# Moving two matmul operands by an odd number of 16-byte lines against the weight buffers

## The chip, the core and the metric

The kernel runs on one core of a Trainium2 chip. The core has a matrix engine (TensorE, PE in the profile; its weight loads are listed apart as PEld), a vector engine (VectorE, DVE), an activation engine (ScalarE, ACT), and queues that start DMA transfers (the SP queue among them). The on-chip memory, SBUF, has 128 partitions; a tile is given by its first byte in each partition. The metric is the device time of one execution in microseconds; lower is better.

## What is computed

A trunk of two layers on 256 tokens of width 2048: layer 0 mixes tokens by pooling, layer 1 by causal attention over one shared K and V, and both attend to 256 memory tokens. Nearly all the work is in dense projections.

```python
def reference(x, mem, w_in, w_out, w_mem_kv, ln_g, ln_b, pool_w, pool_scale, w_kv_shared):
    h = x
    for i in range(DEPTH):                                   # DEPTH = 2
        if i == N_A_LAYERS:                                  # 1
            k_blocks, v_blocks, k_mean = moba_shared_kv(h, w_kv_shared)
        u = h @ w_in[i]                                      # 2048 x 4096
        branch_in, gate_b, mem_q, gate_m = jnp.split(u, split_at, axis=-1)
        if i < N_A_LAYERS:
            branch = multiscale_pool(branch_in, pool_w[i], pool_scale[i])
        else:
            branch = moba_attention(branch_in, k_blocks, v_blocks, k_mean)
        mem_o = memory_attention(mem_q, mem, w_mem_kv[i])
        mixed = jnp.concatenate([branch * jax.nn.silu(gate_b), mem_o * jax.nn.silu(gate_m)], axis=-1)
        h = layer_norm(DEEPNORM_ALPHA * h + mixed @ w_out[i], ln_g[i], ln_b[i])
    return h
```

## The kernel before

Every fp32 number is split into a high part, rounded to the fp32r format that TensorE takes, and a low part, the remainder; a product is the sum of high times high, high times low and low times high. `split` (lines 70 to 73) makes the two parts: ScalarE writes the high one (line 72) and VectorE subtracts it from the source (line 73).

Weights come as items of 512 KB. SP loads each into one of four `raw` buffers, `split` turns it into one of four `wh` and four `wl` buffers of 128 x 1024, and TensorE consumes these. The order of all items is written out once, and TensorE works through it item by item; loads and splits run a fixed number of items ahead.

A matmul has a stationary operand of 128 x 128, which a weight load brings into the array, and a moving operand of up to 512 columns that streams through it. Each matmul here has a weight load of its own. There are four families that read weight buffers together with one of the activation tiles:

- `proj_t` (line 168): the weights are stationary, the activations `xT` or `memT` move. For each of 16 blocks it issues a matmul of 512 columns with `wh` (high and low activations side by side) and one of 256 columns with `wl`. This is the bulk of the kernel.
- `proj_n` (line 194): the activations are stationary (`zT` for the output projections, `memT` for the memory values, `xT` for the shared values), the weights move, 512 columns at a time, in groups of three.
- `pool_mix` (line 564): the weights are stationary, `zT` moves, 256 columns.
- `last` (line 732), for the last output projection: `zT` is stationary, and weights that were split early into `kept` move.

```python
                        if k < KT - 1:
                            mm(acc[n], h[:, kk, s], mov[:, k], k == 0, False)
                        mm(acc[n][:, :T], l[:, kk, s], mov[:, k, :T], False, False)
...
                        mm(acc[t], xh, h[:, kk], first, False)
                        mm(acc[t], xh, l[:, kk], False, False)
                        mm(acc[t], xl, h[:, kk], False, last)
```

(The first three lines are those of `proj_t`, the others those of `proj_n`; `h` and `l` are views of `wh` and `wl`.)

`xm` (line 56) is one region that holds `xT` and `memT`, and later, when these are no longer needed, `kept` and the high and low weights of the shared values (which lie in the place of `memT`). So in the trace `xm` stands for `xT`, `memT` and `kept` alike. All slices that the matmuls take begin at a multiple of 512 bytes from the start of their tile, so the distance between two operands, modulo 512 bytes, is that of their tiles. In the program as built, before the change, the first bytes modulo 512 are: `wh`, `wl`, `raw`, `kept`, `zT` and the attention tiles (`kk`, `qq`, `vv`, `ph`, `pl`) 128; `xT` and `memT` 288, because of `SHIFT = 40` (40 floats, 160 bytes). Counted in lines of 16 bytes, `zT` is level with the weights and `xT` and `memT` lie 10 lines behind them.

Of the kernel before, what the change touches and what calls it, by code (L numbers as in the profile page):

```python
# [12 lines left out]
F32R = mybir.dt.float32r  # L13
# [4 lines left out]
P = 128  # L18
T = 256
D = 2048  # L20
KT = D // P
# [11 lines left out]
BLK = 1024  # L33
RAW_BUFS = 4
WARM = 8
SHIFT = 40
W_BUFS = 4
WARM = 8
SHIFT = 40
LD = 4  # L40
LEAD = 3
LD0 = 8
# [4 lines left out]
def trunk(ctx: ExitStack, tc: tile.TileContext, a: dict, out: bass.AP):  # L47
    nc = tc.nc
    ctx.enter_context(tc.manual_schedule())
    sb = ctx.enter_context(tc.tile_pool(name="sb", bufs=1))  # L50
# [1 line left out]

    xm = sb.tile([P, 2 * KT * 2 * T + 128], F32R, name="xm")
    KX = KT * 2 * T
    xT, memT = (xm[:, SHIFT + i * KX:SHIFT + (i + 1) * KX].rearrange("p (k t) -> p k t", k=KT) for i in range(2))
    kept = [xm[:, i * KX:(i + 1) * KX].rearrange("p (k n) -> p k n", k=KT) for i in range(2)]
    zT = sb.tile([P, KT, 2 * T], F32R, name="zT")  # L60
    res = sb.tile([P, 2, D], F32, name="res")
    ident = mask = psc = eps_t = stats = None

# [189 lines left out]
    def heads_tile(name):  # L253
        return sb.tile([P, 4, 2 * T], F32R, name=name)
# [202 lines left out]
    def fresh(key, make):  # L457

        tiles = []

        def g():
            if not tiles:
                tiles.append(make())
                st[key] = tiles[0]
            return tiles[0]
        return g
# [189 lines left out]
    for grp in range(3):  # L656
        k = fresh("k", lambda: heads_tile("kk"))
# [205 lines left out]
```

## Time and profile before

| | us |
|---|---|
| median of 3 runs | 822.37 (822.33 to 822.89) |
| the profiled execution, its own time | 823.66 |
| its span, first to last instruction | 821.9 |
| TensorE busy | 812.0 |
| VectorE busy | 558.5 |
| ScalarE busy | 396.0 |

The span is what the trace shows; the time of the profiled execution has 1.76 us around it. A matmul's record lasts longer than its share of TensorE, since matmuls overlap: what one costs in a stream is the distance from its start to the start of the next.

### The profile page before, as it was taken

To read this page: it belongs to the slowest core of one execution; us is meant where nothing else is said; L and a number is where in the kernel's file an instruction comes from. 1 tells how busy PE (TensorE), PEld (TensorE's weight loads), DVE (VectorE), ACT (ScalarE), POOL (GpSimd) and SP (SyncE) were. 2 spreads that over 40 slices of the span, in tenths; PEclk is the share of its full clock that TensorE was granted. 3 is DMA by queue.
4 is the path that set the end of the run, shared out by engine and by line. 5 is a ranking of instruction groups with operands and counts; after the bars stand their busy time and mean duration, and the time that the engine had idled before them with its cause. 6 is when DMAs were issued, how large, how long until landed. Compare 5 with 4: busy or idle time off the path is not lost.

```text
span 821.9 us, 11533 instructions
## 1 busy us (share of the span) xinstructions
PE 812.0 (99%) x4444; PEld 702.3 (85%) x4444; DVE 558.5 (68%) x794; ACT 396.0 (48%) x578; POOL 0.2 (0%) x4
## 2 busy tenths in 40 slices
PE   9999999999999999999999999999999999999996
PEld 6888898898888888888898888888888888888885
DVE  5686668657957555697667667566765667658746
ACT  6564545545545434445465445454554445545520
POOL 0000000000000000000000000000000000000000
PEclk9999999999999999999999999999999999999998
DMA  8866555557558666676654554656555555637842
GB/s 324 302 232 205 168 165 180 180 163 227 180 176 292 207 201 192 199 237 197 201 157 152 189 170 157 206 158 198 179 166 168 182 188 167 209 127 232 278 130 103
DMA packets 47164, 159.15 MB, mean 194 GB/s; under 512 B 5375, under 2 KB 7167, under 8 KB 46847
## 3 DMA queue, kind: packets, MB, share of 16 engines
q1 hardware_dynamic: 45792, 155.21, 58.0%
q10 hardware_dynamic: 1316, 3.19, 1.0%
q8 instruction: 35, 0.57, 0.3%
q14 instruction: 21, 0.17, 0.1%
HBM read 156.28 MB, written 2.10 MB: 193 GB/s over the span
## 4 chain that ended last, share of the span: by engine, by line
PE 98%; DVE 1%; DMA 0%; ACT 0%; issue 0%; DVEq 0%; SPq 0%
PE acc L68 89%; PE o L68 4%; PE s L68 2%; PE pt L68 2%; PE pt L363 0%; DMA raw<-in_w_mk 0%; PE pt L313 0%; DVE res L806 0%; PE pt L638 0%; PE o L638 0%; DVE res L787 0%; DVE stats L745 0%; DVE res L744 0%; ACT wh L72 0%; DVEq L859 0%
## 5 line engine op out<-in xcount | busy, mean ns | idle before, releaser
L68 PE MATMUL acc<-xm,wh 128*128 128x512 f32 x1344 | 468.7, 395 | 0.5 <-ACT wh L72 0.5
L73 DVE TENSOR_TENSOR wl<-raw,wh 128x1024 fp32r<-128x1024 f32 (+2 forms) x250 | 295.0, 1186 | 150.0 <-ACT wh L72 149.1
L68 PE MATMUL acc<-xm,wl 128*128 128x256 f32 x1344 | 363.3, 280 | 0.0
L72 ACT ACTIVATE wh<-raw 128x1024 fp32r<-128x1024 f32 (+2 forms) x250 | 255.3, 1028 | 187.3 <-PE acc L68 133.3
L68 PEld LDWEIGHTS acc<-xm,wh 128*128 128x128 f32 x1344 | 248.3, 189 | 49.8 <-ACT wh L72 1.5
L68 PEld LDWEIGHTS acc<-xm,wl 128*128 128x128 f32 x1344 | 253.6, 189 | 7.4 <-DVE wl L73 0.4
L68 PE MATMUL acc<-wh,zT 128*128 128x512 f32 x448 | 140.0, 390 | 0.0
L68 PEld LDWEIGHTS acc<-wh,zT 128*128 128x128 f32 x448 | 84.1, 188 | 17.3
L68 PE MATMUL acc<-wl,zT 128*128 128x512 f32 x224 | 87.2, 389 | 0.0
L68 PE MATMUL acc<-xm 128*128 128x512 f32 x288 | 65.8, 389 | 0.0
L68 PEld LDWEIGHTS acc<-xm 128*128 128x128 f32 x288 | 54.1, 188 | 11.2
L73 DVE TENSOR_TENSOR xm<-raw,xm 128x1024 fp32r<-128x1024 f32 (+2 forms) x41 | 47.7, 1171 | 20.6 <-ACT xm L72 20.4
L221 ACT ACTIVATE fold<-acc 128x256 f32<-128x256 f32 x72 | 27.7, 385 | 62.3 <-PE acc L68 61.1
L72 ACT ACTIVATE xm<-raw 128x1024 fp32r<-128x1024 f32 (+2 forms) x41 | 41.3, 1014 | 19.6 <-PE acc L68 9.8
L68 PEld LDWEIGHTS acc<-wl,zT 128*128 128x128 f32 x224 | 42.1, 188 | 8.5
L222 DVE TENSOR_TENSOR fold<-acc,fold 128x256 f32<-128x256 f32 x72 | 29.4, 418 | 5.4 <-ACT fold L221 5.4
L72 ACT ACTIVATE zT<-zf 128x256 fp32r<-128x256 f32 x32 | 12.9, 414 | 39.6 <-DVE zf L283 35.3
L68 PE MATMUL acc<-xm,zT 128*128 128x256 f32 (+1 forms) x144 | 22.6, 318 | 0.0
L68 PEld LDWEIGHTS acc<-xm,zT 128*128 128x128 f32 x144 | 20.7, 190 | 1.9
L68 PE MATMUL acc<-wh,xm 128*128 128x512 f32 x64 | 21.6, 403 | 0.0
L72 ACT ACTIVATE ph<-pt 128x384 fp32r<-128x384 f32 (+1 forms) x20 | 10.7, 535 | 22.2 <-PE pt L363 13.5
L73 DVE TENSOR_TENSOR zT<-zf,zT 128x256 fp32r<-128x256 f32 x32 | 12.8, 422 | 9.7 <-ACT zT L72 9.7
(124 smaller groups left out, 503.6 us busy)
## 6 DMA issues: line engine op xcount, KB each, us to landing
raw<-in_w_in SPq DMA_DIRECT2D x128, 512.0 KB, 3.5
raw<-in_w_out SPq DMA_DIRECT2D x64, 512.0 KB, 4.3
raw<-in_w_sk SPq DMA_DIRECT2D x24, 512.0 KB, 4.5
raw<-in_w_sv SPq DMA_DIRECT2D x24, 512.0 KB, 3.3
raw<-in_w_mv SPq DMA_DIRECT2D x14, 512.0 KB, 5.6
raw<-in_w_mk SPq DMA_DIRECT2D x12, 512.0 KB, 3.3
raw<-in_xT SPq DMA_DIRECT2D x4, 512.0 KB, 4.8
res<-in_x ACTq DMA_DIRECT2D x2, 1024.0 KB, 5.4
```

Source lines behind the costliest of these rows:

```text
L68: nc.tensor.matmul(o, l, r, start=start, stop=stop)
L72: nc.scalar.activation(hi, src, AF.Copy)
L73: nc.vector.tensor_sub(lo, src, f(hi))
L221: nc.scalar.activation(dst, acc[:, T:], AF.Copy)
L222: nc.vector.tensor_add(dst, acc[:, :T], dst)
```

## The change

```diff
-SHIFT = 40
+LINE = 4
+KEPT = 8
+SHIFT = KEPT + 44
@@
     xT, memT = (xm[:, SHIFT + i * KX:SHIFT + (i + 1) * KX].rearrange("p (k t) -> p k t", k=KT) for i in range(2))
-    kept = [xm[:, i * KX:(i + 1) * KX].rearrange("p (k n) -> p k n", k=KT) for i in range(2)]
-    zT = sb.tile([P, KT, 2 * T], F32R, name="zT")
+    kept = [xm[:, KEPT + i * KX:KEPT + (i + 1) * KX].rearrange("p (k n) -> p k n", k=KT) for i in range(2)]
+    zT = sb.tile([P, KX + 2 * LINE], F32R, name="zT")[:, LINE:LINE + KX].rearrange("p (k t) -> p k t", k=KT)
```

`zT` gets a border of 16 bytes on both sides, so it begins at 144 modulo 512, and every tile that is allocated after it (`raw`, `wh`, `wl`, the attention tiles, the constants) lies 32 bytes further on: 160. `kept` moves by 32 bytes along with them, to 160. `xT` and `memT` move by 48 bytes, to 336. The result, in lines of 16 bytes:

| operand | against the weights before | after |
|---|---|---|
| `xT`, `memT` | 10 lines behind | 11 lines behind |
| `zT` | level | 1 line ahead |
| `kept` | level | level |
| attention tiles | level among themselves | level among themselves |
| `xT` against the shared values' weights in `memT`'s place | level | level |

No instruction is added, removed or moved on any engine: the rows of the program, apart from line numbers, are the same, with the same waits.

## Rows read from the trace of the kernel before

**Rows 1.** The page: its head, part 1, part 4 by engine.
```profile
span 821.9 us, 11533 instructions
...
PE 812.0 (99%) x4444; PEld 702.3 (85%) x4444; DVE 558.5 (68%) x794; ACT 396.0 (48%) x578; POOL 0.2 (0%) x4
...
PE 98%; DVE 1%; DMA 0%; ACT 0%; issue 0%; DVEq 0%; SPq 0%
```

**Rows 2.** Groups by form: count, busy us, mean ns, idle before, releaser.
```profile
L68 PE MATMUL acc<-xm,wh 128*128 128x512 f32 x1344 | 468.7, 395 | 0.5 <-ACT wh L72 0.5
L68 PE MATMUL acc<-xm,wl 128*128 128x256 f32 x1344 | 363.3, 280 | 0.0
L73 DVE TENSOR_TENSOR wl<-raw,wh 128x1024 fp32r<-128x1024 f32 x234 | 284.7, 1223 | 145.2 <-ACT wh L72 144.3
...
L68 PE MATMUL acc<-wh,zT 128*128 128x512 f32 x448 | 140.0, 390 | 0.0
L68 PE MATMUL acc<-wl,zT 128*128 128x512 f32 x224 | 87.2, 389 | 0.0
...
L68 PE MATMUL acc<-wh,xm 128*128 128x512 f32 x64 | 21.6, 403 | 0.0
...
L68 PE MATMUL acc<-wl,xm 128*128 128x512 f32 x32 | 12.6, 393 | 0.0
...
L68 PE MATMUL acc<-xm,zT 128*128 128x256 f32 x96 | 11.7, 283 | 0.0
...
L68 PE MATMUL acc<-xm,zT 128*128 128x512 f32 x48 | 11.0, 389 | 0.0
...
L68 PE MATMUL o<-zT,wh 128*128 128x256 f32 x24 | 4.5, 283 | 0.0
```

**Rows 3.** Timeline of PE, 6 to 9 us: start, length, what.
```profile
6.16 0.63 PE L68 MATMUL acc<-xm,wh 128*128 128x512 f32 x1
...
8.72 0.63 PE L68 MATMUL acc<-xm,wh 128*128 128x512 f32 x1
```

**Rows 4.** Timeline of PE in `proj_t`, 641 to 646 us.
```profile
641.13 0.39 PE L68 MATMUL acc<-xm,wh 128*128 128x512 f32 x1
641.36 0.28 PE L68 MATMUL acc<-xm,wl 128*128 128x256 f32 x1
...
645.98 0.39 PE L68 MATMUL acc<-xm,wh 128*128 128x512 f32 x1
```

**Rows 5.** Timeline of the weight loads, same stretch.
```profile
641.13 0.19 PEld L68 LDWEIGHTS acc<-xm,wl 128*128 128x128 f32 x1
641.36 0.19 PEld L68 LDWEIGHTS acc<-xm,wh 128*128 128x128 f32 x1
```

**Rows 6.** Timeline of PE in the output projection of layer 0, `zT` stationary.
```profile
269.78 0.39 PE L68 MATMUL acc<-wh,zT 128*128 128x512 f32 x1
...
274.99 0.39 PE L68 MATMUL acc<-wh,zT 128*128 128x512 f32 x1
```

**Rows 7.** Timeline of PE in `pool_mix` (`zT` moves), 256 to 258 us.
```profile
256.69 0.40 PE L68 MATMUL o<-zT,wh 128*128 128x256 f32 x2
...
257.77 0.40 PE L68 MATMUL acc<-wh,zT 128*128 128x512 f32 x1
```

**Rows 8.** Timeline of PE in the shared values, `xT` stationary, 508 to 530 us.
```profile
508.03 21.95 PE L68 MATMUL acc<-xm 128*128 128x512 f32 x96
529.81 0.39 PE L68 MATMUL acc<-xm,wh 128*128 128x512 f32 x1
```

**Rows 9.** Timeline of PE in the memory values, `memT` stationary, 14 to 19 us.
```profile
14.53 0.40 PE L68 MATMUL o<-wh,xm 128*128 128x512 f32 x1
...
18.73 0.39 PE L68 MATMUL acc<-xm,wh 128*128 128x512 f32 x1
```

**Rows 10.** Windows: busy us and counts of PE, PEld, DVE, ACT, POOL; clock, DMA share, GB/s.
```profile
5.00:10.00 5.00, 4.68 (x15) 3.93 (x15) 4.11 (x10) 4.06 (x9) 0.00 (x0) 1.00 0.96 327
10.00:13.00 3.00, 3.00 (x18) 2.65 (x18) 1.24 (x2) 1.69 (x2) 0.00 (x0) 1.00 1.00 406
20.00:52.00 32.00, 32.00 (x162) 26.93 (x161) 23.39 (x29) 17.61 (x21) 0.00 (x0) 1.00 0.77 259
122.00:172.00 50.00, 50.00 (x290) 43.94 (x289) 35.72 (x44) 25.78 (x38) 0.00 (x0) 1.00 0.54 169
262.00:336.00 74.00, 74.00 (x328) 61.23 (x328) 42.90 (x44) 30.09 (x31) 0.00 (x0) 1.00 0.65 203
```

More of the change, by code (lines that the diff above doesn't have):

```diff
@@ L35 @@
 WARM = 8
-SHIFT = 40
+LINE = 4
+KEPT = 8
+SHIFT = KEPT + 44
 W_BUFS = 4
 WARM = 8
-SHIFT = 40
+LINE = 4
+KEPT = 8
+SHIFT = KEPT + 44
 LD = 4
```

## The prediction

> **What bounds the kernel now.** I read the page first: TensorE is busy 812.0 of 821.9 us and 98% of the chain that ended last is TensorE [rows 1]. VectorE and ScalarE wait for it more than it waits for them. So the time is the sum of the distances from one matmul's start to the next, and the only question is what a matmul costs in the stream. The groups by form give the counts, but their mean durations (395 ns for 512 columns) overlap and can't be added [rows 2]; the timeline gives the distances, and I took them over long stretches, because its starts are rounded to 10 ns.
>
> Four families have operands that the change moves against each other, and there each distance is longer than the columns alone explain:
>
> - `proj_t`, 10 lines apart: 14 pairs of 512 + 256 columns from 641.13 to 645.98, 346.4 ns a pair [rows 4].
> - `zT` stationary, level: 23 matmuls of 512 columns from 269.78 to 274.99, 226.5 ns each [rows 6].
> - `pool_mix`, level: nine matmuls of 256 columns from 256.69 to 257.77, 120.0 ns each [rows 7].
> - the memory values, 10 lines apart the other way round: 18 matmuls from 14.53 to 18.73, 233.3 ns each [rows 9].
>
> [...]
>
> The load starts when the matmul before its own starts: 641.13 and 641.36 in both timelines [rows 4, 5]. So one matmul's moving operand and the next one's stationary operand are read at the same time, and all the distances that I have are even numbers of lines (0, 10). [...]
>
> **The change part by part.** Nothing is added, removed or reordered, so the only cost or gain is in these distances, and in what the new addresses do to other engines.
>
> Loads that the change touches: `proj_t` 2 x 1344 = 2688; `zT` stationary 448 + 224, and in `last` 96 + 48, together 816; `pool_mix` 3 groups of 24 + 12 = 108; the memory values 96 under the name `acc` and the same again under `pt` and `o` together, 192 [rows 2]. The shared values stay level and keep their 226.9 ns (96 matmuls from 508.03 to 529.81, three times) [rows 8]; attention stays level too. These are the control.
>
> The trace of before shows no odd distance, so the price there is bounded from both sides. Least: no collision at all, the columns alone. That gives 1344 x 26.4 = 35.5 us, 816 x 13.2 = 10.8 us, 108 x 13.3 = 1.4 us, 192 x 20.0 = 3.8 us, together 51.5 us. Most, on the other side: every load pays what the memory values pay, 20.0 ns, 6.7 ns more than now on 2688 + 816 + 108 = 3612 loads: 24.2 us lost. In the middle lies nothing at all.
>
> I take half of the full gain, 25.8 us. The nearest rows are the even ones, and none of them says which way an odd one goes; but if a collision is two reads in the same set of lines, odd against even is the distance at which the two stay apart when both advance a line in the same time. Against all of it going: the price differs between level and 10 lines the one way but not the other, so the two reads don't keep step exactly, and part of the loads will slide back into step.
>
> [...]
>
> Other engines: the source and target of a split move together by 32 bytes, so VectorE and ScalarE see the same relations as before, except for what is written to `zT`, `xT` and `memT`. I cost that at nothing. An item takes TensorE 8 x 346.4 ns = 2.77 us, and VectorE's share of it is 1.223 us [rows 2]; in the `proj_t` stretch VectorE is busy 35.72 of 50 us and the DMA share is 0.54 [rows 10]. With 8% less time per item these become 77% and 0.58: cover is left. If VectorE were 10% slower on the new addresses, it would still be at 85%. Only the start has no cover: from 5 to 13 us the DMA share is 0.96 to 1.00 [rows 10], so a faster TensorE may wait for data there, and the 8 us give back at most 8% of themselves, 0.6 us. From 20 to 52 us it is 0.77, with room.
>
> The sum stands against the profiled execution's own time: 823.66 - 25.8 = 797.9 us. That execution was 1.29 us above the median of the runs shown, so for the median I say 796.5.
>
> **The rivals.** *All of it goes.* [...] Time 822.4 - 51.5 = 770.9 us.
>
> *Only a little goes* (2 to 13 us): the odd distance helps `zT`, which was exactly level, and hardly `proj_t`, where 10 lines already pay the same as level. `zT` and `pool_mix` alone give up to 12.2 us. Time 810 to 820 us.
>
> *The distance doesn't matter.* [...] For it: level and 10 lines behind cost the same. [...] Time 822.4 us. [...]
>
> *The odd distance is worse.* [...] `proj_t` carries it: 2688 loads. If all pay the 20.0 ns, the time is 822.4 + 24.2 = 846.6 us. It decides against the change as soon as a load costs 0.5 ns more on average (3612 x 0.46 ns = 1.6 us, 0.2%).
>
> **How the numbers follow.** About 0.2%, 1.6 us, is what a measurement of this kernel can tell from no change. I give half of the gain, 13 to 39 us, 0.36; nearly all of it (39 to 52) 0.15; a little of it 0.13; nothing 0.14; worse 0.22, of which 0.10 by less than 8 us. The likeliest is 796.5, with its own range of 783 to 809. To hold 8 in 10 the range reaches down into the case of all of it, to 777, which leaves out about 0.06, and up to 830, which leaves out the greater half of the worse case, 0.12. Faster 0.15 + 0.36 + 0.13 = 0.64, same 0.14, slower 0.22.
>
> **What would show each step.** In the timeline after, a `proj_t` pair at about 333 ns, `zT` stationary at 220, `pool_mix` at 113, the memory values near 223; the shared values unchanged at 227, and VectorE's 1223 ns for a split unchanged. The prediction is wrong if the pair stays at 346 (the distance doesn't matter) or grows, or if the pair falls to 320 (all of it). If TensorE's distances shrink but the span doesn't, waits for DMA must have grown, first before 52 us. If the shared values move as well, the cause is not the distance between the two operands.

## The result, and the profile after

The changed kernel is slower: 827.90 us (826.68 to 828.89, 4 runs) against 822.58 (822.33 to 822.89, 4 runs), ratio 1.0064, 95% interval 1.0051 to 1.0076. The forecast was 796.5, faster.

The page after (head, part 1, part 4 by engine) has the shape of [rows 1]:

```profile
span 827.1 us, 11533 instructions
...
PE 817.2 (99%) x4444; PEld 703.5 (85%) x4444; DVE 558.8 (68%) x794; ACT 396.1 (48%) x578; POOL 0.2 (0%) x4
...
PE 98%; DVE 1%; DMA 0%; ACT 0%; issue 0%; DVEq 0%; SPq 0%
```

TensorE is busy 5.2 us longer and the span is 5.2 us longer; VectorE and ScalarE do the same work in the same time. So nothing new is waited for: the matmuls themselves stand further apart. The timeline of PE after, in the stretches of [rows 4], [rows 6], [rows 8] and [rows 9], says where:

```profile
14.86 0.40 PE L71 MATMUL o<-wh,xm 128*128 128x512 f32 x1
...
19.01 0.39 PE L71 MATMUL acc<-xm,wh 128*128 128x512 f32 x1
...
269.63 0.62 PE L71 MATMUL acc<-wh,zT 128*128 128x512 f32 x2
...
277.85 0.39 PE L71 MATMUL acc<-wh,zT 128*128 128x512 f32 x1
...
510.75 22.24 PE L71 MATMUL acc<-xm 128*128 128x512 f32 x96
532.82 0.40 PE L71 MATMUL acc<-xm,wh 128*128 128x512 f32 x1
...
644.66 0.40 PE L71 MATMUL acc<-xm,wh 128*128 128x512 f32 x1
...
649.56 0.40 PE L71 MATMUL acc<-xm,wh 128*128 128x512 f32 x1
```

| family | before, ns | after, ns | how read after |
|---|---|---|---|
| `proj_t`, a pair | 346.4 | 350.0 | 14 pairs, 644.66 to 649.56 |
| `zT` stationary | 226.5 | 228.3 | 36 matmuls, 269.63 to 277.85 |
| `pool_mix` | 120.0 | 117.8 | 9, 258.14 to 259.20 |
| memory values | 233.3 | 230.6 | 18, 14.86 to 19.01 |
| shared values | 226.9 | 229.9 | 96, 510.75 to 532.82 |

The reader is to see two things. No family came near the 333, 220, 113 and 223 ns of the forecast; two paid a little less and three a little more, and the big one is among these. And the shared values moved by 3.0 ns, although their two operands are level before and after: they were meant as the control.

### The profile page after: what moved, and what is told of

Read it like the earlier page. It is cut to its first block, busy times and chain, and to the rows that moved or that the text cites. A ratio compares the mean times of both kernels' runs of the same rounds, so it can differ in the third digit from the quotient of the medians.

```text
span 827.1 us, 11533 instructions
## 1 busy us (share of the span) xinstructions
PE 817.2 (99%) x4444; PEld 703.5 (85%) x4444; DVE 558.8 (68%) x794; ACT 396.1 (48%) x578; POOL 0.2 (0%) x4
## 4 chain that ended last, share of the span: by engine, by line
PE 98%; DVE 1%; DMA 0%; ACT 0%; issue 0%; DVEq 0%; SPq 0%
PE acc L71 89%; PE o L71 4%; PE s L71 2%; PE pt L71 2%; PE pt L366 0%; DMA raw<-in_w_mk 0%; PE pt L316 0%; DVE res L809 0%; PE o L641 0%; PE pt L641 0%; DVE res L790 0%; DVE stats L748 0%; DVE res L747 0%; ACT wh L75 0%; DVEq L862 0%
```

## The experiments

Distances in nanoseconds below are read like those in the table, from one start to another over the count between.

**Quiet streams.** After the kernel's last matmul, streams were added that no other engine runs beside; their results go nowhere.

```diff
+    def stream(w, m, go, n=48):
+        o = ps.tile([P, 512], F32, name="acc", bufs=4)
+        W, M = still(w, m)      # views of xm: W begins w lines, M m lines past an even place
+        for k in range(n):
+            go(o, W[:, k % 32], M[:, k % KT], k == 0, k == n - 1)
+    stream(0, 0, lambda *x: nc.tensor.matmul(*x))
...
```

> The kernel before, with streams of matmuls added at its end, when the other engines are done; their results go nowhere, and their time comes on top, so only the distances between matmuls count. Each stream is 48 matmuls of 512 columns with a weight load each, both operands out of the same region, the moving one m lines and the stationary one w lines of 16 bytes past an even place; four more streams are of 32 pairs of 512 + 256 columns. Theory D (distance): level streams cost 226.7 ns a matmul wherever they begin, (m,w) = (0,0), (1,1), (11,11) alike, and odd distances cost more, 228 to 232. Theory P (place): what begins at an odd line costs more by itself, so (1,1) and (11,11) cost about 230 like the shared values after, and (1,0), (11,0) more than (0,0), while (0,2), (2,0), (0,4), (4,0) cost 226.7. Theory T (traffic): the differences come from the other engines' reads and writes, so here all streams cost the same, and pairs cost the same for m = 0, 1, 10, 11.

The timeline of PE in this run, one row a stream (L820 is level at an even line, L821 level at line 1, L822 has the stationary operand a line on, L823 the moving one; L824 has the stationary one two lines on, L825 the moving one):

```profile
828.46 11.04 PE L820 MATMUL acc<-xm 128*128 128x512 f32 x48
839.34 11.20 PE L821 MATMUL acc<-xm 128*128 128x512 f32 x48
850.38 11.06 PE L822 MATMUL acc<-xm 128*128 128x512 f32 x48
861.28 11.28 PE L823 MATMUL acc<-xm 128*128 128x512 f32 x48
872.39 11.36 PE L824 MATMUL acc<-xm 128*128 128x512 f32 x48
883.59 11.36 PE L825 MATMUL acc<-xm 128*128 128x512 f32 x48
```

From start to start over 48: level at an even line 226.7, level at an odd line 230.0, the stationary operand a line on 227.1, the moving one a line on 231.5, two lines either way 233.3. With nothing else running these are the kernel's prices to a nanosecond (the shared values' 226.9 and 229.9, the memory values' 233.3 before), so theory T, traffic, falls. The pairs cost 347.2 level, 346.9 at 10 lines, 349.7 at 11 and 346.9 at 1. Neither D nor P is enough: level operands cost more at an odd line (against D), but two lines, an even place, cost 233.3 where P expects 226.7, the stationary operand one line on costs next to nothing, and a pair at 1 line costs what it costs at 10 (against P).

**Each half alone, and neither.**

```diff
 zt_only:  -SHIFT = KEPT + 44
           +SHIFT = KEPT + 40
 xt_only:  -    zT = sb.tile(...)[:, LINE:LINE + KX]...
           +    zT = sb.tile(...)[:, 2 * LINE:2 * LINE + KX]...
 shift32:  both lines
```

> The changed kernel with xT and memT put back to 10 lines behind the weights; zT stays 1 line ahead. Theories D and P: proj_t pairs back to 346.4 ns, shared values back to 226.9, zT stationary stays at 228.3 and pool_mix at 117; of the 5.3 us lost about 0.7 stay, 823.3 us. Theory T (32 bytes of shift of all other buffers do it): proj_t and the shared values stay where they are after, 827 us.

> The changed kernel with zT put back level with the weights; xT and memT stay 11 lines behind. Theories D and P: zT stationary back to 226.7 ns, pool_mix to 120; proj_t pairs stay near 350 ns. Shared values (level with each other, both at an odd line): 230 by theory P, 226.9 by theory D. About 827 us. Theory T: zT stationary stays at 228.3.

> The changed kernel with both put back: zT level, xT and memT 10 lines behind, everything 32 bytes further on than before. Theories D and P: all distances as before, 822.6 us, ratio within 0.1% of 1. Theory T, or if 32 bytes of place matter by themselves: up to the whole 5.3 us stay, 824 to 828 us.

Measured: `zT` alone 823.68, ratio 1.0016 (1.0007 to 1.0025); `xT` alone 826.76, 1.0053 (1.0039 to 1.0067); neither 822.50, 1.0004 (0.9996 to 1.0013). The two halves add up to the whole, 0.0069 against 0.0064, and 32 bytes for everything cost nothing that can be told. With `xT` alone, the shared values:

```profile
510.58 22.24 PE L71 MATMUL acc<-xm 128*128 128x512 f32 x96
532.66 0.40 PE L71 MATMUL acc<-xm,wh 128*128 128x512 f32 x1
```

With `xT` alone 24 `zT` matmuls from 272.01 to 277.45 are 226.7 ns each, as before; the shared values, level at an odd line, cost 230.0. So those 3 ns belong to where `xT` and `memT` begin, not to their distance.

**Maps of the distance.** Are odd and even two classes, and is there a distance at which the price goes?

> The kernel before with streams added at its end, as in the first of the quiet runs: 48 matmuls of 512 columns each, the moving operand 0 to 31 lines past the even place of the stationary one, then the stationary one 1 to 31 lines past that of the moving one. Theory D (the distance alone sets the price): the price repeats with the distance, even and odd distances form two classes, and m lines ahead equals 32 - m lines ahead the other way round. [...] If a distance exists at which the two reads pass each other, some place costs under 220.

> The kernel before with streams added at its end: 32 of the pairs of proj_t, 512 + 256 columns, at 0 to 31 lines; 32 of the triples of proj_n with the stationary operand at 0 to 31 lines; level streams that begin at line 1, 2, 3, 4, 8, 16 and 21; level streams with a stationary operand of 64 and of 32 columns. Theory D: pairs at odd places one price, at even places another. [...] Level streams: by a rule of place, lines 1, 3 and 21 cost 230 and lines 2, 4, 8 and 16 226.7; by distance alone all 226.7. [...]

The timeline of the first map; L835 + m is the stream whose moving operand is m lines on:

```profile
841.61 11.28 PE L836 MATMUL acc<-xm 128*128 128x512 f32 x48
852.72 11.37 PE L837 MATMUL acc<-xm 128*128 128x512 f32 x48
863.93 11.36 PE L838 MATMUL acc<-xm 128*128 128x512 f32 x48
...
997.95 11.05 PE L850 MATMUL acc<-xm 128*128 128x512 f32 x48
1008.84 11.08 PE L851 MATMUL acc<-xm 128*128 128x512 f32 x48
1019.76 11.28 PE L852 MATMUL acc<-xm 128*128 128x512 f32 x48
1030.88 11.37 PE L853 MATMUL acc<-xm 128*128 128x512 f32 x48
```

Line 1 costs 231.5 and line 17 231.7 (11.11 and 11.12 us); the same holds for all 16 places of the moving operand against the 16 that follow, within 0.8 ns. So its price repeats every 16 lines, 256 bytes. The places of the stationary operand do so too, with one exception: 1 line costs 233.1 (11.19 us, 1187.00 to 1198.19) and 17 lines 226.9 (10.89 us, 1365.13 to 1376.02), where the first quiet run had 227.1 for 1 line. Within the period there is no odd and even class: 15 and 16 lines of the moving operand cost 226.9 and 227.5, 4 lines 229.2, 2 and 3 233.5 and 233.1. No place of 63 is under 226.7. Nor is there one price for all places away from level: several lie between, at 229 to 232.

The pairs (L835 + m again) and the narrow streams of the second map:

```profile
942.50 11.26 PE L845 MATMUL acc<-xm 128*128 128x512 f32 x64
953.60 11.36 PE L846 MATMUL acc<-xm 128*128 128x512 f32 x64
964.79 11.45 PE L847 MATMUL acc<-xm 128*128 128x512 f32 x64
...
1621.30 11.19 PE L906 MATMUL acc<-xm 128*64 128x512 f32 x48
1632.33 11.28 PE L907 MATMUL acc<-xm 128*32 128x512 f32 x48
1643.45 11.08 PE L908 MATMUL acc<-xm 128*128 128x512 f32 x48
```

A pair costs 346.9 at 10 lines (11.10 us for 32), 349.7 at 11 and 352.8 at 12; over 32 places it lies between 346.8 and 353.5, with 346.8 to 347.1 at 1, 2, 9, 10, 14 and 16. On this map the pairs of the kernel before stood at the floor, and 11 lines cost 3 ns more. The 32 triples repeat the first map's prices of the stationary operand's places within 0.3 ns, save 1 line, which costs 226.8 here. Level at line 1 is 230.0 (1544.45 to 1555.49), at line 2 227.7 (1555.49 to 1566.42). And level, 64 and 32 columns of stationary operand cost 229.8 and 231.7, not less than the 226.7 of 128: the price does not fall with the columns that a load brings in.

**The maps put to the test in the kernel.**

```diff
-SHIFT = 40
+SHIFT = 64      (e7), 16 (e8), 36 (e9)
```

> The kernel before with xT and memT 16 lines (256 bytes) behind the weights instead of 10; nothing else moves. Theory M (the kernel's time is the sum of the quiet prices over its families): proj_t pairs 346.9 ns instead of 346.8 (+0.1 us), the memory values 226.7 instead of 233.2 (192 matmuls, -1.25 us), shared values unchanged at 226.9; together -1.1 us, ratio 0.9986, 821.2 us. Theory E (even distances alike, odd ones dear): no change, 822.3 us.

> The kernel before with xT and memT 4 lines (64 bytes) behind the weights. Theory M: proj_t pairs 353.5 ns, 1344 x 6.7 = +9.0 us, memory values 233.2 as before; 831.3 us, ratio 1.011. Theory E: an even distance, no change, 822.3 us.

> The kernel before with xT and memT 9 lines (144 bytes) behind the weights. Theory M: proj_t pairs 347.0 ns (+0.3 us), memory values 233.4 (0), shared values level but at an odd line, 230.0 instead of 226.7 (288 matmuls, +0.95 us); 823.5 us, ratio 1.0015. Theory E: an odd distance, so as with 11 lines, 826.8 us, ratio 1.0053.

Measured: 16 lines 827.53, ratio 1.0057 (1.0044 to 1.0070); 4 lines 827.38, 1.0059 (1.0047 to 1.0072); 9 lines 822.68, 0.9997 (0.9988 to 1.0006). Theory E falls on all three: two even distances lose as much as 11 lines did, and an odd one loses nothing. Theory M misses all three as well: its 1.0015 for 9 lines lies outside the interval, 4 lines have the right sign and half the size, and 16 lines have the wrong sign. With 16 lines, in `proj_t`, two groups of six pairs, a microsecond apart:

```profile
692.65 0.40 PE L68 MATMUL acc<-xm,wh 128*128 128x512 f32 x1
...
694.73 0.40 PE L68 MATMUL acc<-xm,wh 128*128 128x512 f32 x1
...
695.76 0.40 PE L68 MATMUL acc<-xm,wh 128*128 128x512 f32 x1
...
697.88 0.40 PE L68 MATMUL acc<-xm,wh 128*128 128x512 f32 x1
```

The first six pairs take 346.7 ns each, as on the map, the next six 353.3; over the whole kernel the pairs without a pause take 351.8 on average. The level pairs had shown 347.2 in the first quiet run and 352.8 in the second map (11.29 us, 830.40 to 841.69). So one place can have two prices, and the kernel with 16 lines shows both.

> The kernel before with streams added at its end: the pairs of proj_t at 16, 10, 9 and 11 lines, each four times, after four different forerunners. Theory H (a place has more than one repeating pattern, and what ran before decides which): the pairs at 16 lines cost 346.9 ns after some forerunners and about 353 after others, as the kernel with 16 lines did; at 10, 9 and 11 lines 346.8, 347.0 and 350 after all four. If pairs at 16 lines cost 346.9 after all four, the kernel's 351.4 has another cause, the other engines' traffic first.

Rows of its timeline; L836 and L840 are pairs at 16 lines, L837 a stream with the stationary operand two lines on, L839 and L855 streams with the moving operand 7 lines on, L856 pairs at 9 lines:

```profile
840.32 11.45 PE L836 MATMUL acc<-xm 128*128 128x512 f32 x64
851.61 11.36 PE L837 MATMUL acc<-xm 128*128 128x512 f32 x48
...
874.09 11.26 PE L839 MATMUL acc<-xm 128*128 128x512 f32 x48
885.19 11.46 PE L840 MATMUL acc<-xm 128*128 128x512 f32 x64
...
1052.39 11.04 PE L855 MATMUL acc<-xm 128*128 128x512 f32 x48
1063.27 11.26 PE L856 MATMUL acc<-xm 128*128 128x512 f32 x64
```

At 16 lines the pairs cost 353 after all four forerunners (11.29 us for 32, 840.32 to 851.61), and at 10, 9 and 11 lines 346.9, 347.0 and 350 after all four. For the pairs at 16 lines this run alone does not show two prices; beside the map it does: 346.9 there, after pairs at 15 lines, 353 here, both in quiet. For the stream at 7 lines it does alone: 231.3 after pairs at 16 lines (L839), 226.7 after pairs at 9 lines (L855). So 353 in the kernel needs no traffic to explain it. What picks the pattern is not settled.

**What the price goes with.**

> The kernel before with streams added at its end: bf16 operands of 512 columns at 0, 1, 2, 4, 7 and 10 lines; fp32r with 384 and with 256 columns at 0, 1, 2, 7 and 10 lines; fp32r with a stationary operand of 64 columns at four places. [...] The earlier run has shown that 64 and 32 columns of stationary operand pay no less (229.8 and 231.7), so one cycle for each line of the load has fallen; with 64 columns other places are expected between 226 and 234.

The timeline of this run (bf16 at 1 line and at 2 lines; fp32r with 384 columns at 10 lines; with 256 columns level, L864, and at 7 lines, L867; a stationary operand of 64 columns with the moving one 10 lines on, L871):

```profile
839.59 10.52 PE L854 MATMUL acc<-gate 128*128 128x512 bf16 x47
849.95 10.52 PE L855 MATMUL acc<-gate 128*128 128x512 bf16 x47
...
924.78 8.48 PE L863 MATMUL acc<-xm 128*128 128x384 f32 x48
933.10 5.91 PE L864 MATMUL acc<-xm 128*128 128x256 f32 x48
938.84 5.87 PE L865 MATMUL acc<-xm 128*128 128x256 f32 x48
...
950.15 5.66 PE L867 MATMUL acc<-xm 128*128 128x256 f32 x48
955.64 5.79 PE L868 MATMUL acc<-xm 128*128 128x256 f32 x48
...
983.39 11.05 PE L871 MATMUL acc<-xm 128*64 128x512 f32 x48
994.28 11.27 PE L872 MATMUL acc<-xm 128*64 128x512 f32 x48
```

A bf16 stream takes 10.36 us for 48 matmuls (one record is missing), 215.8 ns, at every place tried; in fp32r the cheapest place of the maps costs 226.7. So what fp32r takes beyond 215.8 does not come with every change of the stationary operand, as bf16 changes it for each matmul too. That the smaller volume is the reason is not shown: a bf16 load is also shorter, in the trace of before 150 ns (from 2.01 us on) against 330 in fp32r (from 5.94 us on). With 384 columns of fp32r a matmul takes 173.3 ns at 10 lines (8.32 us for 48) and 177.3 level (8.51 us). With 256 columns it takes 119.6 level (5.74 us), 119.0, 116.7 and 117.3 at 1, 2 and 10 lines, and 114.4 at 7 lines (5.49 us). With 64 columns of stationary operand all four places lie in the range expected: 230.0 level, 230.8 and 226.9 with the moving operand 2 and 10 lines on, 231.3 with the stationary one 10 lines on. At the last three places 128 columns cost 233.4, 234.3 and 233.2, so there fewer columns pay less, by 2 to 7.5 ns, but in no way that follows the number of lines.

**A version from the maps.** Only the memory values stood at a dear place before, so `memT` alone was moved.

```diff
-    xT, memT = (xm[:, SHIFT + i * KX:SHIFT + (i + 1) * KX]... for i in range(2))
+    xT, place1, memT = (xm[:, s:s + KX]... for s in (SHIFT, SHIFT + KX, 68 + KX))
-        return [memT[:, 4 * (j % 4) + ...
+        return [place1[:, 4 * (j % 4) + ...
```

> The kernel before, with memT alone moved from 10 to 17 lines behind the weights (17 is 1 modulo 16); xT stays at 10, and the shared values' weights keep a place level with xT. From the quiet streams: memory values 226.8 ns instead of 233.2 (192 matmuls, -1.25 us), the 128 pairs of the memory keys 347.2 instead of 346.8 (+0.05 us); everything else unchanged. 821.4 us against 822.6, ratio 0.9985. If a quiet stream doesn't tell what the kernel pays (as it didn't for 16 lines), the memory values stay above 230 and the time stays.

```profile
14.19 0.39 PE L68 MATMUL o<-wh,xm 128*128 128x512 f32 x1
...
18.27 0.39 PE L68 MATMUL acc<-xm,wh 128*128 128x512 f32 x1
...
47.24 0.40 PE L68 MATMUL o<-wh,xm 128*128 128x512 f32 x1
...
51.44 0.40 PE L68 MATMUL acc<-xm,wh 128*128 128x512 f32 x1
```

The first 18 matmuls take 4.08 us, 226.7 ns each, as foretold. The same 18 of a later item take 4.20 us, 233.3 each: half of the 192 matmuls kept the old price. The time is 822.74, ratio 1.0002 (0.9993 to 1.0011), against 0.9985 expected: no gain that can be told.

**The same traces, summed.** What the medians can't tell, the traces can. Six of them run the kernel before (five with streams behind it). The first 40 matmuls, among them the pairs of [rows 3] at 640 ns each, take 10.1 to 12.2 us in these six; from there to the transposition near the end all six agree within 0.02 us. The two ends of this stretch, before and with `memT` at 17 lines:

```profile
13.14 0.39 PE L68 MATMUL pt<-wh,xm 128*128 128x512 f32 x1
...
814.80 0.27 PE L794 MATMUL pt<-ident,cc 128*5 128x128 f32 x1 [2.84 <-DVE cc L791]
...
12.82 0.39 PE L68 MATMUL pt<-wh,xm 128*128 128x512 f32 x1
...
813.95 0.27 PE L794 MATMUL pt<-ident,cc 128*5 128x128 f32 x1 [2.84 <-DVE cc L791]
```

That is 801.66 and 801.13 us. The difference of each kernel from the 801.66, in us, with every distance put to the family of its first matmul:

| kernel | all | `proj_t` | `zT` stationary | shared values | memory values |
|---|---|---|---|---|---|
| the change | +4.7 | +3.6 | +1.0 | +0.9 | -0.5 |
| `zT` alone | +0.8 | 0.0 | +1.0 | 0.0 | 0.0 |
| `xT` alone | +4.0 | +3.6 | 0.0 | +0.9 | -0.5 |
| neither | +0.1 | 0.0 | 0.0 | 0.0 | +0.1 |
| 16 lines | +5.1 | +5.8 | -0.1 | 0.0 | -0.6 |
| 4 lines | +5.2 | +5.4 | 0.0 | -0.1 | +0.1 |
| 9 lines | 0.0 | -0.9 | 0.0 | +0.9 | +0.1 |
| `memT` at 17 lines | -0.5 | 0.0 | 0.0 | 0.0 | -0.6 |

`pool_mix` adds -0.2 in the first two rows. The halves add up here too. The 9 lines did not leave everything as it was: `proj_t` takes 0.9 us less and the shared values 0.9 more. And `memT` at 17 lines is 0.5 us faster than the kernel before, less than half of what was foretold, and too little for the medians to show. Each changed kernel has one trace, so the 0.02 us is known for the kernel before alone; but as that kernel repeats itself so closely, what ran before a matmul, and not chance, seems to pick the pattern.

## Why the prediction was wrong, point by point

- **What bounds the kernel** was right. TensorE's distances are the time, before and after; no wait for DMA, VectorE or ScalarE took part, and the cover that the prediction counted was never needed.
- **That the places of the two operands count** was right: quiet streams move between 226.7 and 234.5 ns when one operand's place alone is changed, while a load's own record stays at 187 to 189 ns in the first quiet run, whatever the place. That the two reads collide is the author's picture; the runs show the distances, not a collision. Whether the whole price, or only its change with the place, comes from the load beside the matmul is open, as no matmul was run without a load.
- **The terms of the sum** were not shown. No run shows the 26.4, 13.2, 13.3 and 20.0 ns from which the 51.5 us are added up and the 8% less time per item follows: they are distances less a time for the columns alone that was not measured. In its place the runs showed 215.8 ns for 512 columns in bf16, in fp32r 226.7 ns or more at all 63 places of the first map, and 346.8 or more for a pair. Nor do the distances speak for one price of a load. 64 columns of stationary operand pay 229.8 ns and 32 pay 231.7, against 226.7 for 128. And in the trace of before the 512 columns of a `proj_t` pair take 230 ns from start to start and the 256 columns 117 (medians; 641.13 to 641.36 in [rows 4] is one such step), where `zT` stationary takes 226.5 and `pool_mix` 120.0: the sums agree, 346.4 and 346.5, the parts do not.
- **"I take half of the full gain, 25.8 us"** is the step that sank the forecast, with its reason, "odd against even is the distance at which the two stay apart". The gain there was none: over all places of a 256-byte period the quiet pairs lie between 346.8 and 353.5 ns, and 10 lines was among the cheapest. In the place of the term stand these, summed over the traces: `proj_t` +3.6 us (346.4 to 350.0 ns a pair in the stretches shown), 720 matmuls of 512 columns with `zT` stationary +1.0, shared values +0.9, memory values -0.5, `pool_mix` -0.2, together +4.7 with a rest of -0.1. Of the 5.2 us in the span the other 0.5 lies before the first memory value (0.3, well within the 2 us by which the start of the kernel before varies) and behind that transposition (0.2).
- **The control** was misjudged: "the shared values stay level and keep their 226.9 ns". They stayed level and rose to 229.9. Level operands cost 230.0 at lines 1 and 3, 231.1 at line 21 and 226.7 to 227.7 at lines 0, 2, 4, 8 and 16, so where both begin counts too. The prediction had named this sign itself: "If the shared values move as well, the cause is not the distance between the two operands." By the maps it is not the distance alone.
- **The rivals.** "The odd distance is worse" had the sign, and the place that carries it, `proj_t`; its price of 6.7 ns a load was four times too large (1.5 ns, half of 3 ns a pair). That an odd distance by itself costs more fits `zT` at most: the shared values stayed level, and in `proj_t` 9 lines gain 0.9 us while 4 and 16 lose more than 11 (5.4 and 5.8 against 3.6 us).
- **The size of the range** followed from the wrong bound: the full gain of 51.5 us supposed that all of these terms can go. In fp32r no quiet stream of 512 columns took less than 226.7 ns a matmul, and no quiet pairs less than 346.8 ns. The measured 827.9 lies inside the stated 777 to 830, but only because the range was wide: it gave 0.10 to a loss of less than 8 us, and nothing of its mechanism leads there.

What stays open: what makes the pattern of 16 lines, and what decides between 346.9 and 353 ns for a pair at 0 or 16 lines; and whether bf16 takes its 215.8 ns for its smaller volume or for its shorter load.

## What to carry to other kernels

When matmuls stand back to back, their distance may move with the operands' places by a few nanoseconds each way (here from 226.7 to 234.5 ns for 512 columns of fp32r), but that it moves is no sign of how far it can fall: measure the lowest price over a whole period of places in a stream at the kernel's end before counting on a gain. A number that seems to fit a mechanism deserves one test that varies the count (here the columns of a load: 226.7, 229.8 and 231.7 ns for 128, 64 and 32). And a place that is cheap in a quiet stream can be dear in the kernel, and in one part of the kernel but not in another, so the last word is the kernel's own distances, summed over the whole trace.

## What the runs showed of the hardware that was not expected

- The price of a matmul in fp32r depends on both operands' first bytes, with a period of 256 bytes but for places that have two prices: 512 columns cost 226.7 to 234.5 ns, a pair of 512 and 256 columns 346.8 to 353.5.
- One arrangement can repeat in more than one pattern: pairs at 16 lines 346.9 or 353 ns, and in one and the same run a stream at 7 lines 231.3 (11.10 us for 48, 874.09 to 885.19) or, after pairs at 9 lines, 226.7 (10.88 us, 1052.39 to 1063.27). With `memT` at 17 lines half of the memory values paid 226.7 and half 233.3 in one kernel.
- Fewer columns of stationary operand cost more when level (226.7, 229.8 and 231.7 ns for 128, 64 and 32) and less at three other places (234.3 and 226.9 for 128 and 64 with the moving operand 10 lines on). In bf16 512 columns took 215.8 ns at all six places.
- From the 41st matmul on, six executions of the kernel before took the same 801.66 us within 0.02; nearly all of what differs between them lies in the first 40 matmuls, 10.1 to 12.2 us.
